# A two-layer hybrid decoder trunk: queries scaled with the keys, exchanged halves read in one product, paired Y tiles, a new order of steps

## The chip, the cores and the metric

One core of one Trainium2 chip runs the whole program. The time is the device time of one execution in microseconds; three executions of the kernel before are given by their median. Work is spread over TensorE (PE), VectorE (DVE), ScalarE (ACT), GpSimd (POOL) and SyncE (SP, which issues most DMAs). Each has its own instruction stream and works it off in the order in which the program was written.

## What is computed

Two layers on x (512 x 1024, float32). Each mixes tokens by three attentions of one normalised input and then channels by a gated convolution block:

```python
for i in range(DEPTH):                                   # DEPTH = 2
    h = rms_norm(x, attn_norm[i])
    qa, ka, va, qb, kb, vb, qc, kc, vc, gates = split(h @ w_in[i])
    # q and k of A, B, C: rms_norm per head, then rotary:
    #   concat([x1 * c - x2 * s, x2 * c + x1 * s])
    ya = moba_attention(qa, ka, va)                      # 4 heads of 64
    yb = sliding_window_sink_attention(qb, kb, vb, sinks[i])   # 8 heads on 2 kv heads
    yc = differential_attention(qc, kc, vc, lam, subln)  # 4 heads, two softmax maps of 32
    g = sigmoid(gates.reshape(B, S, 3, D))
    merged = g[..., 0, :] * (ya @ w_pa) + g[..., 1, :] * (yb @ w_pb) + g[..., 2, :] * (yc @ w_pc)
    x = x + merged @ w_out[i]
    h = rms_norm(x, mlp_norm[i])
    u = causal_depthwise_conv(h @ w_up[i], conv_w[i], conv_b[i])   # width 3
    gate_u, val_u = split(u, 2)                          # 2816 each
    x = x + (silu(gate_u) * val_u) @ w_down[i]
```

## The kernel before

**Products.** A float32 product of activations and weights is made as three products of reduced operands: each side is split into a high part and the rest, and high x high, high x rest and rest x high are summed. A weight tile of 128x1024 comes by DMA into one of two `raw` buffers; ACT casts it to `whi`, and DVE (one instruction) or POOL (four pieces of 256) subtracts to get `wlo` (`w_prep`, L639). The tile's `raw` buffer is free for the next transfer when both are done. Activations have the same two parts, `h0k` and `h1k` for k = 0 to 7. PE sums into one of four PSUM banks `d`; two banks `tp` take transposes and attention outputs, two banks `s` scores.

**Stages of a layer.** A list `ORDER` (layer 0) or `ORDER1` (layer 1) orders the blocks of dense products of the attention half: `Q` for a branch's q, k and v columns (blocks qk of 4 tiles and v of 2), `g` for half a gate (4 tiles), `p` for half an output projection. Then come the two halves of w_out, eleven `up` blocks (4 tiles each, with convolution and SiLU at their evacuation) and two `down` blocks of 11 tiles. "vC" below is branch C's v block, "gC0" the first half of C's gate, and a number behind a dot is the layer.

**Attention.** For each branch the projected q and k are rotated, scaled and split (`prep`, L903, with `rope`, L887), transposed on PE, multiplied to scores, masked, exponentiated (`soft`, L1073), transposed again, multiplied with v, and gathered into Y tiles (`gather`, L1230), the left side of the projections. Between these steps data goes PE, PSUM, ACT or DVE, PE.

**Who runs when.** The program is a set of generators ("threads"), each asking for its next step on one engine. A planner (`Estimate`, from L177, and the loop at the end of `trunk`) keeps a clock per engine from a table of durations and picks, step by step, the thread that goes on; threads have priorities (`P_...`). The dense blocks are the thread of lowest priority and fill PE where no attention step is ready. So every constant at the head of the file and every entry of the cost table moves instructions.

**Normalisation.** A branch that stands in `ORDER` ahead of the first gate works on the input before it is normalised, and its outputs are scaled at evacuation by `rn`, the reciprocal norms (`RAW_BR`). Behind the last of them `renorm` (L583) makes the normalised parts: for each k a DVE product, an ACT cast to `h0k` and a DVE subtraction to `h1k`. They overwrite the parts that the raw branches read. In the same way the first `up` block reads un-normalised h; its outputs get a row of reciprocal norms `ROW` at evacuation (`evac_up`, L1391, where the product is written back into the PSUM bank), while `renorm` makes the parts for the ten others.

**Softmax.** `rstd_tb` (L799) makes reciprocal norms of q and k on POOL: `RS` and `NRS` for q (with the score scale and its negative), `RK` for k. k is scaled by `RK` after rotary, q is not: its scale goes into the exponential, exp(RS * s + nb), with nb = NRS * max(s).

Of the kernel before, what the change touches and what calls it, by code (L numbers as in the profile page):

```python
# [26 lines left out]
LOCK = True  # L27
ORDER = ('QC', 'QA', 'gC0', 'QB', 'gC1', 'gA0', 'gA1', 'pC0', 'gB0', 'pC1', 'pA0', 'gB1', 'pA1', 'pB0', 'pB1')
CAP = 3
POOL_LEAD = 2.5  # L30
POOL_BIAS = -1000000000.0
RAWUP = 1
RENORM = 1.5
EXTRA = ({'C': 0, 'A': 6, 'B': 0}, {'C': 13, 'A': 3, 'B': 35})
GROOM = (0, 4)
PRING = 3
UNPARK = 6
PTMAX = 6
QUOTA = (6, 6)
HURRY = 1  # L40
P_HURRY = 2
P_SCORE = 4.5
P_TRANS = 2.5
P_VALUE = 3.4
P_SOFT = 1.9
P_SPREAD = 0.2
P_GATHER = 0.7
P_SUBLN = 0.7
P_SQUASH = 2.1
P_MOVE = 3.6  # L50
P_PREP = 5
TOL = 0.05
COPY = 0.2
SCALE = 1
# [5 lines left out]
MAJ_OUT = 3  # L60
MAJ_DOWN = 0
MAJ_LAST = 3
FINE = 1
SPILL = 8

# [108 lines left out]
class Estimate:  # L174
    SEM = 0.16

    def __init__(self):  # L177
        self.clock = {"PE": 0.0, "ACT": 0.0, "DVE": 0.0, "POOL": 0.0, "SP": 0.3, "DGE": 0.0, "DMA": 0.0}
        self.table = None
        self.mode = None  # L180
        self.written = {}
        self.used = {}
        self.pred = {}
        self.rings = {}
        self.lock = LOCK
        self.port = {"DVE": deque(maxlen=24), "POOL": deque(maxlen=24)}
# [52 lines left out]
    def note(self, key, op, args, kw):
# [9 lines left out]
        ins = [x for x in aps if not any(x is o for o in outs)]  # L249
        t = self.clock[key]  # L250
        for x in ins:
            t = max(t, self.written.get(x.tensor.name, 0.0) + self.SEM)
        for o in outs:
            nm = o.tensor.name
            if key != "PE" and op != "dma_start":
                t = max(t, self.written.get(nm, 0.0) + (self.SEM if nm in self.written else 0.0))
            if nm[:2] in ("h0", "h1"):
                t = max(t, self.used.get(nm, 0.0) + self.SEM)
            if nm in self.pred:
                t = max(t, self.used.get(self.pred.pop(nm), 0.0) + self.SEM)  # L260
        if op == "dma_start":
# [5 lines left out]
        else:  # L267
            two = False
            if self.lock and key in ("DVE", "POOL"):
# [6 lines left out]
            if two:  # L276
                for s, e in self.port["POOL" if key == "DVE" else "DVE"]:
                    if s <= t < e:
                        t = e
            end = t + self.cost(key, op, out, ins, kw, args)  # L280
            self.clock[key] = end
            if two:
                gap = 0.05 if key == "POOL" else 0.0
                self.port[key].append((t + gap, end - gap))
# [4 lines left out]
        for o in outs:  # L289
            self.written[o.tensor.name] = max(self.written.get(o.tensor.name, 0.0), end)  # L290
# [40 lines left out]
def trunk(ctx: ExitStack, tc: tile.TileContext, out: bass.AP, a: dict):  # L331
# [448 lines left out]
    RW, SS, V, RS, NRS, RK, Y, SIG, M, MH = {}, {}, {}, {}, {}, {}, {}, {}, {}, {}  # L780

    def alloc_raw(br, l):
        RW[br] = [slots.get() for _ in range(2)]
        RK[br] = small.tile([128, TB, NK[br]], F32, name="rk" + br, bufs=1)
        RS[br] = small.tile([128, TB, NQ[br]], F32, name="rq" + br, bufs=1)
        NRS[br] = small.tile([128, TB, NQ[br]], F32, name="nrq" + br, bufs=1)
# [12 lines left out]
    def rstd_tb(br, t, g0, g1):  # L799
        nq = NQ[br]  # L800
        v = small.tile([128, 16], F32, name="vv", bufs=3)[:, :g1 - g0]
        nc.vector.tensor_scalar(v, SS[br][:, g0:g1], 1.0 / DH[br], EPS, op0=OP.mult, op1=OP.add)
        r = small.tile([128, 16], F32, name="rr", bufs=3)[:, :g1 - g0]
        nc.gpsimd.tensor_tensor(r, v, mhalf[:, :g1 - g0], op=OP.pow)
        sc = DH[br] ** -0.5
        if g0 < nq:
            nc.gpsimd.tensor_scalar(RS[br][:, t, :], r[:, :nq], sc, None, op0=OP.mult)
            nc.gpsimd.tensor_scalar(NRS[br][:, t, :], r[:, :nq], -sc, None, op0=OP.mult)
        if g1 > nq:
            nc.gpsimd.tensor_copy(RK[br][:, t, :], r[:, max(nq - g0, 0):])  # L810

    def evac_qk(br, key):
        def f(t, ps):
            if br in RAW_BR[key // 2]:
                nc.scalar.activation(raw_tb(br, t), ps, AF.Copy, scale=RN[key][:, t:t + 1])
            else:
                nc.scalar.copy(raw_tb(br, t), ps)
# [69 lines left out]
    def rope(br, t, sv, dv, mv, q0, q1):  # L887
# [8 lines left out]
        nc.vector.tensor_mul(mv[:, :, :, :h], sv[:, :, :, h:], tab(t2, 0, h))  # L896
# [760 lines left out]
```

## Time and profile before

| what | us |
|---|---|
| median of three runs | 1584.74 (1582.8 to 1584.83) |
| the profiled execution | 1583.99 |
| its span in the trace | 1582.1 |
| PE busy | 1544.0 |
| mean granted clock of PE | 0.999 of full speed |

The profiled execution is 0.75 us under the median. An instruction's row has its start and duration; in brackets stands how long its engine was idle before it and which operation released it. Every instruction carries the line of one helper (L168), so rows are told apart by tiles and shapes. A row of grouped instructions ends with the total idle time just before them. Matmuls overlap: the row of one 512-column matmul lasts some 0.39 us, but a new one can start before the last ends.

### The profile page before, as it was taken

To read this page: it belongs to the slowest core of one execution; us is meant where nothing else is said; L and a number is where in the kernel's file an instruction comes from. 1 tells how busy PE (TensorE), PEld (TensorE's weight loads), DVE (VectorE), ACT (ScalarE), POOL (GpSimd) and SP (SyncE) were. 2 spreads that over 40 slices of the span, in tenths; PEclk is the share of its full clock that TensorE was granted. 3 is DMA by queue.
4 is the path that set the end of the run, shared out by engine and by line. 5 is a ranking of instruction groups with operands and counts; after the bars stand their busy time and mean duration, and the time that the engine had idled before them with its cause. 6 is when DMAs were issued, how large, how long until landed. Compare 5 with 4: busy or idle time off the path is not lost.

```text
span 1582.1 us, 21228 instructions
## 1 busy us (share of the span) xinstructions
PE 1544.0 (98%) x7584; PEld 1281.9 (81%) x7584; DVE 1048.0 (66%) x2211; ACT 800.8 (51%) x1566; POOL 338.9 (21%) x455
## 2 busy tenths in 40 slices
PE   8999999999999999999999999999999999999999
PEld 6977888877878888888888787888888788888887
DVE  4798878887576665543249887887776855665231
ACT  7566686764444444333146666766734544444210
POOL 3465443431010000000034564443300200000000
PEclk9999999999999999999999999999999999999999
DMA  5522523214223333333332224322242233223331
GB/s 176 154 68 79 173 68 94 80 54 135 90 83 107 89 98 107 107 98 127 95 114 69 66 79 160 107 67 61 73 159 88 72 106 107 80 86 101 120 120 53
DMA packets 115496, 157.22 MB, mean 99 GB/s; under 512 B 18880, under 2 KB 71104, under 8 KB 115392
## 3 DMA queue, kind: packets, MB, share of 16 engines
q1 hardware_dynamic: 102768, 153.19, 31.3%
q10 hardware_dynamic: 12624, 2.69, 0.9%
q8 instruction: 60, 0.98, 0.3%
q14 instruction: 44, 0.36, 0.1%
HBM read 144.84 MB, written 11.01 MB: 99 GB/s over the span
## 4 chain that ended last, share of the span: by engine, by line
PE 77%; DVE 14%; ACT 4%; DMA 2%; POOL 2%; issue 1%; SPq 0%; ACTq 0%; DVEq 0%; POOLq 0%
PE d L168 70%; PE tp L168 6%; DVE slot L168 5%; DVE temp L168 4%; ACT slot L168 2%; PE s L168 1%; DVE h L168 1%; ACT whi L168 1%; DVE s L168 1%; DMA raw<-in_w_up 1%; DVE wlo L168 1%; POOL rr L168 1%; DVE nb L168 1%; DMA slot<-in_c_cs 0%; ACT h L168 0%
## 5 line engine op out<-in xcount | busy, mean ns | idle before, releaser
L168 PE MATMUL d<-h,whi 128*128 128x512 f32 x2176 | 681.2, 394 | 4.0 <-DVE temp L168 2.7
L168 PEld LDWEIGHTS d<-h,whi 128*128 128x128 f32 x2176 | 398.6, 188 | 84.5 <-ACT temp L168 5.4
L168 PE MATMUL d<-h,wlo 128*128 128x512 f32 x1088 | 424.8, 390 | 0.0
L168 ACT CAST whi<-raw 128x1024 fp32r<-128x1024 f32 x246 | 256.2, 1052 | 280.2 <-PE d L168 136.3
L168 DVE TENSOR_TENSOR wlo<-raw,whi 128x1024 fp32r<-128x1024 f32 x175 | 213.5, 1233 | 257.9 <-ACT whi L168 257.5
L168 POOL TENSOR_TENSOR wlo<-raw,whi 128x256 fp32r<-128x256 f32 x284 | 225.2, 823 | 351.9 <-ACT whi L168 315.2
L168 PE MATMUL d<-slot,whi 128*128 128x512 f32 x864 | 267.0, 390 | 0.0
L168 PEld LDWEIGHTS d<-h,wlo 128*128 128x128 f32 x1088 | 204.2, 188 | 44.0
L168 PE MATMUL d<-whi,h 128*128 128x512 f32 (+1 forms) x768 | 205.9, 346 | 0.6 <-ACT h L168 0.6
L168 PEld LDWEIGHTS d<-slot,whi 128*128 128x128 f32 x864 | 161.1, 188 | 32.8
L168 DVE SCALAR_TENSOR_TENSOR temp<-d,packed,temp 128x511 f32<-128x511 f32 (+1 forms) x176 | 127.8, 747 | 63.4 <-ACT temp L168 60.3
L168 PE MATMUL d<-slot,wlo 128*128 128x512 f32 x432 | 168.2, 389 | 0.0
L168 PEld LDWEIGHTS d<-whi,h 128*128 128x128 f32 x768 | 134.8, 192 | 15.8 <-ACT h L168 1.0
L168 ACT CAST slot<-tp 128x256 fp32r<-128x256 f32 (+4 forms) x308 | 108.2, 379 | 70.8 <-PE tp L168 64.6
L168 PE MATMUL d<-wlo,h 128*128 128x256 f32 (+1 forms) x384 | 131.1, 341 | 0.2 <-DVE wlo L168 0.2
L168 ACT ACTIVATE temp<-d,packed 128x512 f32<-128x512 f32 x88 | 67.9, 773 | 86.1 <-PE d L168 79.4
L168 PE MATMUL d<-whi,slot 128*128 128x512 f32 x352 | 108.6, 389 | 0.0
L168 POOL TENSOR_TENSOR rn<-nvs,mhalf 128x4 f32<-128x4 f32 x3 | 3.0, 1008 | 482.4 <-DVE nvs L168 482.4
L168 DVE TENSOR_TENSOR slot<-slot,d 128x512 f32<-128x512 f32 x80 | 54.6, 685 | 73.9 <-PE d L168 71.2
L168 PEld LDWEIGHTS d<-slot,wlo 128*128 128x128 f32 x432 | 81.1, 188 | 17.0
L168 DVE TENSOR_TENSOR slot<-tp,slot 64x128 fp32r<-64x128 f32 (+4 forms) x180 | 76.0, 425 | 25.7 <-ACT slot L168 24.1
L168 ACT CAST slot<-temp 128x256 fp32r<-128x256 f32 (+2 forms) x140 | 58.1, 454 | 56.7 <-DVE temp L168 56.5
(113 smaller groups left out, 1784.8 us busy)
## 6 DMA issues: line engine op xcount, KB each, us to landing
raw<-in_w_up SPq DMA_DIRECT2D x176, 256.0 KB, 3.4
raw<-in_w_in SPq DMA_DIRECT2D x82, 512.0 KB, 3.7
raw<-in_w_down SPq DMA_DIRECT2D x44, 512.0 KB, 3.9
raw<-in_w_out SPq DMA_DIRECT2D x16, 512.0 KB, 4.6
x_spill<-slot SPq DMA_DIRECT2D x8, 512.0 KB, 3.9
b_parked<-slot SPq DMA_DIRECT2D x8, 512.0 KB, 5.3
slot<-b_parked SPq DMA_DIRECT2D x8, 512.0 KB, 5.8
raw<-in_w_pb SPq DMA_DIRECT2D x8, 512.0 KB, 3.7
```

The source lines that it names most:

```text
L168: r = f(*args, **kw)
```

## The change

1. **Reciprocal norms.** `RS`, `NRS` and `RK` become one tile `RQK`, written by the power on POOL itself. q is scaled together with k after rotary, in one wider product. The masked reduction of scores gives nb directly (with a factor -sqrt(dh) and a minimum), so that the product that made nb goes, and the exponential's scale is the constant -1.
2. **Rotary.** The two products of exchanged halves become one that reads the halves in exchanged order; q and k are evacuated in an arrangement of parts for it.
3. **Y tiles of B** are paired so that each of two evacuations of `gather` moves 64x2x128 where four moved 64x128.
4. **First up block.** The row product goes to an SBUF slot (`UR`) and not back into the PSUM bank; the activation and the convolution's two steps read the slot.
5. **Differential scale.** Where DVE scales the second map, reciprocal and lambda are applied in one instruction.
6. **Planner.** Latencies per engine, ready times by parts of a tile, other costs, and other constants and orders. Ahead of the first gate now stands only C, so the normalised parts are made between vC and gC0 in both layers.

```diff
-ORDER = ('QC', 'QA', 'gC0', 'QB', 'gC1', 'gA0', 'gA1', 'pC0', 'gB0', 'pC1', 'pA0', 'gB1', 'pA1', 'pB0', 'pB1')
-CAP = 3
+ORDER = ('QC', 'gC0', 'QA', 'gA0', 'QB', 'gC1', 'gA1', 'pC0', 'pC1', 'gB0', 'pA0', 'pA1', 'gB1', 'pB0', 'pB1')
+CAP = 4
...
-RENORM = 1.5
+RENORM = 0.5
...
-TOL = 0.05
+TOL = -0.2
...
-ORDER1 = ('QC', 'QA', 'gC0', 'QB', 'gC1', 'pC0', 'gA0', 'pC1', 'gB0', 'gA1', 'gB1', 'pA0', 'pA1', 'pB0', 'pB1')
+ORDER1 = ('QC', 'gC0', 'QA', 'gC1', 'QB', 'gA0', 'pC0', 'pC1', 'gA1', 'gB0', 'pA0', 'gB1', 'pA1', 'pB0', 'pB1')
...
-    SEM = 0.16
+    SEM = {"PE": 0.08, "ACT": 0.05, "DVE": 0.034, "POOL": 0.08, "SP": 0.1}
+    LAG = {"PE": 0.163, "ACT": 0.1, "DVE": 0.084, "POOL": 0.045}
...
-        r = small.tile([128, 16], F32, name="rr", bufs=3)[:, :g1 - g0]
-        nc.gpsimd.tensor_tensor(r, v, mhalf[:, :g1 - g0], op=OP.pow)
-        sc = DH[br] ** -0.5
-        if g0 < nq:
-            nc.gpsimd.tensor_scalar(RS[br][:, t, :], r[:, :nq], sc, None, op0=OP.mult)
-            nc.gpsimd.tensor_scalar(NRS[br][:, t, :], r[:, :nq], -sc, None, op0=OP.mult)
-        if g1 > nq:
-            nc.gpsimd.tensor_copy(RK[br][:, t, :], r[:, max(nq - g0, 0):])
...
+        nc.gpsimd.tensor_tensor(o, v.rearrange("p (q n) -> p q n", n=h),
+                                mhalf[:, :g1 - g0].rearrange("p (q n) -> p q n", n=h), op=OP.pow)
...
-        nc.vector.tensor_mul(mv[:, :, :, :h], sv[:, :, :, h:], tab(t2, 0, h))
-        nc.vector.tensor_mul(mv[:, :, :, h:], sv[:, :, :, :h], tab(t2, h, 2 * h))
+        x = bass.AP(tensor=sv.tensor, offset=sv.offset + h,
+                    ap=[list(sv.ap[0]), [2 * h, (q1 - q0) * n], [-h, 2], [1, h]])
+        nc.vector.tensor_mul(mv, x, tab(t2, 0, 2 * h))
...
-            nc.vector.tensor_mul(kv, kv, RK[br][:, t, p * nk:(p + 1) * nk, None].to_broadcast([128, nk, d]))
+            if br == "B":
+                r5 = rot[:, :320].rearrange("p (n d) -> p n d", d=d)
+                nc.vector.tensor_mul(r5, r5, RQK[br][:, t, p, :, None].to_broadcast([128, 5, d]))
+            else:
+                r4 = rot[:, :256].rearrange("p (q n d) -> p q n d", q=2, d=d)
+                nc.vector.tensor_mul(r4, r4, RQK[br][:, t, :, p * nk:(p + 1) * nk, None].to_broadcast([128, 2, nk, d]))
...
-                nc.vector.tensor_tensor_reduce(s_, s_, mask, 1.0, -3e38, OP.add, OP.max, job["mx"][:, m:m + 1])
-            nb = job["nb"][:, m0:m1]
-            nc.vector.tensor_mul(nb, job["mx"][:, m0:m1], NRS[br][:, t, g0 + m0:g0 + m1])
+                nc.vector.tensor_tensor_reduce(s_, s_, mask, -DH[br] ** 0.5, 3e38, OP.add, OP.min, job["nb"][:, m:m + 1])
...
-                                     scale=RS[br][:, t, g0 + m:g0 + m + 1], accum_out=job["den"][:, m:m + 1])
+                                     scale=-1.0, accum_out=job["den"][:, m:m + 1])
...
-            for i in range(4 if br == "B" else 2):
...
+            for i in range(2):
+                r = slice(i * 64, i * 64 + 64)
+                if br == "B":
+                    x = ps.rearrange("p (a i c) -> p a i c", a=2, i=2)[r, :, i, :]
+                    dst.append((two(Y[br][2 * p])[r, :, sl], two(Y[br][2 * p + 1])[r, :, sl], x))
...
             if blk < RAWUP:
-                nc.vector.tensor_mul(ps, ps, ROW[2 * l + 1][:, :512])
+                if c % 2 == 0:
+                    UR[c // 2] = slots.get()
+                r = UR[c // 2][:, (c % 2) * 512:(c % 2) * 512 + 512]
+                nc.vector.tensor_mul(r, ps, ROW[2 * l + 1][:, :512])
+                ps = r
```

TensorE has the same number of instructions before and after, 7558. VectorE's go from 2209 to 1985, ScalarE's from 1417 to 1369, GpSimd's from 460 to 380. Three places show how the streams move. A name is the tile's with a running number; `mx`, `nb` are the softmax's maximum and bias, `temp` and `slot` working tiles.

ScalarE at the end of vC in layer 0, before: behind the four evacuations of v (`slot21_22 <- d, rn`) stand the casts of two weight tiles and the evacuation of vA.

```order
L168 ACTIVATE slot21_22_524<-d_526,rn_129 128x256
L168 COPY slot23_24_602<-tp1_10_519 128x512
L168 ACTIVATE slot21_22_524<-d_539,rn_129 128x256
L168 ACTIVATE slot21_22_524<-d_552,rn_129 128x256
L168 ACTIVATE slot21_22_524<-d_565,rn_129 128x256
L168 CAST whi_643<-raw_502 128x1024
L168 CAST whi_709<-raw_583 128x1024
L168 ACTIVATE slot26_27_655<-d_657,rn_129 128x256
L168 ACTIVATE slot26_27_655<-d_670,rn_129 128x256
```

VectorE at the same place, before: the rest of v, one weight tile, then branch C's rotary.

```order
L168 SCALAR_TENSOR_TENSOR slot22_23_525<-d_565,rn_129,slot21_22_524 128x256
L168 TENSOR_TENSOR wlo_644<-raw_502,whi_643 128x1024
L168 TENSOR_TENSOR temp3_7_726<-slot11_12_201,slot16_17_504 128x256
L168 TENSOR_TENSOR temp1_8_727<-slot11_12_201,slot16_17_504 128x8x16 x2
L168 TENSOR_TENSOR temp3_7_726<-temp3_7_726,temp1_8_727 128x256
L168 TENSOR_TENSOR temp3_7_726<-temp3_7_726,rkC_203 128x128
```

The same place after, first on ScalarE, then on VectorE. Behind the four evacuations stand the cast of one weight tile and those to `h00` and the following parts:

```order
L169 ACTIVATE slot21_22_506<-d_508,rn_129 128x256
L169 ACTIVATE slot21_22_506<-d_521,rn_129 128x256
L169 ACTIVATE slot21_22_506<-d_534,rn_129 128x256
L169 ACTIVATE slot21_22_506<-d_547,rn_129 128x256
L169 CAST whi_633<-raw_484 128x1024
L169 CAST h00_113<-slot24_25_606 128x512
L169 CAST h01_114<-slot25_26_608 128x512
L169 CAST h02_115<-slot26_27_618 128x512
L169 CAST h03_116<-slot27_28_626 128x512
```

```order
L169 SCALAR_TENSOR_TENSOR slot22_23_507<-d_547,rn_129,slot21_22_506 128x256
L169 TENSOR_TENSOR wlo_634<-raw_484,whi_633 128x1024
L169 TENSOR_TENSOR h10_121<-slot24_25_606,h00_113 128x512
L169 TENSOR_TENSOR h11_122<-slot25_26_608,h01_114 128x512
L169 TENSOR_TENSOR h12_123<-slot26_27_618,h02_115 128x512
```

What moved: the casts to `h00` and on, and the subtractions to `h10` and on, which gC0's first matmuls read, came twenty and more rows later before, and now stand directly at vC's end.

ScalarE between the first and second up block of layer 0, before and after. `whi` is the cast of a weight tile, `h05` to `h07` the casts of the normalised parts; `slot` are the block's outputs.

```order
L168 CAST slot27_208_5134<-temp1_67_5090 128x512
L168 CAST slot13_209_5137<-temp2_68_5100 128x512
L168 CAST whi_5140<-raw_5035 128x1024
L168 CAST h05_4646<-slot17_207_5082 128x512
L168 CAST whi_5183<-raw_5077 128x1024
L168 CAST h06_4647<-slot29_210_5172 128x512
L168 CAST h07_4648<-slot10_211_5178 128x512
L168 CAST whi_5219<-raw_5147 128x1024
```

```order
L169 CAST slot23_210_4902<-temp3_67_4855 128x512
L169 CAST slot29_211_4905<-temp2_68_4866 128x512
L169 CAST whi_4908<-raw_4802 128x1024
L169 CAST whi_4947<-raw_4842 128x1024
L169 CAST whi_4982<-raw_4915 128x1024
L169 CAST h06_4412<-slot18_212_4966 128x512
L169 CAST h07_4413<-slot17_213_4974 128x512
L169 CAST whi_5015<-raw_4951 128x1024
```

What moved: `h06` and `h07` stood ahead of the cast of the third block's first tile, `whi_5219`; now they stand behind its counterpart, `whi_4982`, whose `raw` buffer is the one that POOL's `wlo_4909` (the third tile of the second block) frees.

VectorE in a softmax of branch C in layer 0, before and after (`ISA` is the masked reduction, followed by its write of the row value):

```order
L168 ISA s0_1_881,mx2_878<-s0_1_881,mfull_86 128x128
L168 ISA mx2_878 128x1
L168 TENSOR_TENSOR nb2_879<-mx2_878,nrqC_205 128x1
L168 ISA s1_2_883,mx2_878<-s1_2_883,mfull_86 128x128
L168 ISA mx2_878 128x1
L168 TENSOR_TENSOR nb2_879<-mx2_878,nrqC_205 128x1
```

```order
L169 TENSOR_TENSOR temp3_13_811<-temp3_13_811,rqkC_203 128x256
L169 ISA s0_1_825,nb2_823<-s0_1_825,mfull_86 128x128
L169 ISA nb2_823 128x1
L169 ISA s1_2_827,nb2_823<-s1_2_827,mfull_86 128x128
L169 ISA nb2_823 128x1
```

What moved: the product that made `nb` is no longer between the reductions and the exponential, and the scaling ahead of them is twice as wide.

## Rows read from the trace of the kernel before

**Rows 1.** Part 1 of the page: busy time of each engine, share, instructions.
```profile
PE 1544.0 (98%) x7584; PEld 1281.9 (81%) x7584; DVE 1048.0 (66%) x2211; ACT 800.8 (51%) x1566; POOL 338.9 (21%) x455
```

**Rows 2.** Windows: length, busy PE, PEld, DVE, ACT, POOL; clock, DMA, GB/s.
```profile
39.00:94.00 55.00, 51.03 (x342) 45.45 (x341) 42.89 (x113) 30.70 (x74) 26.00 (x34) 1.00 0.46 134
94.00:366.00 272.00, 264.31 (x1428) 220.30 (x1428) 233.65 (x682) 184.92 (x455) 123.34 (x171) 0.99 0.30 88
...
797.00:844.00 47.00, 46.11 (x310) 42.23 (x309) 25.82 (x50) 21.48 (x40) 21.33 (x29) 1.00 0.37 107
844.00:874.00 30.00, 28.16 (x147) 22.54 (x146) 29.07 (x80) 20.69 (x52) 13.89 (x17) 1.00 0.26 72
874.00:1144.00 270.00, 262.77 (x1416) 217.87 (x1415) 220.28 (x650) 187.39 (x460) 125.57 (x172) 1.00 0.29 87
```

**Rows 3.** Waits of PE: who released it, us in total, times, longest.
```profile
PE tp L168 <- DVE slot L168: 16.9, 26, 2.9
...
PE d L168 <- DVE temp L168: 2.7, 4, 1.0
```

**Rows 4.** Groups by operation and shape: busy, mean ns | idle before, released by.
```profile
L168 PE MATMUL tp<-identf,slot 128*128 128x128 f32 x352 | 55.6, 277 | 8.9 <-DVE slot L168 7.4 <-DVE nss L168 1.0 <-ACT slot L168 0.3
...
L168 DVE TENSOR_TENSOR temp<-slot,slot 128x128 f32<-128x128 f32 x96 | 38.9, 446 | 0.0
...
L168 PE MATMUL tp<-identr,slot 128*128 128x128 f32 x320 | 37.7, 240 | 3.1 <-DVE slot L168 2.1 <-ACT slot L168 0.6
...
L168 DVE TENSOR_TENSOR temp<-slot,slot 128x256 f32<-128x256 f32 x48 | 25.8, 537 | 1.1 <-POOL slot L168 1.1
...
L168 DVE TENSOR_TENSOR nb<-mx,nrqC 128x1 f32<-128x1 f32 x64 | 14.6, 227 | 2.2
...
L168 DVE TENSOR_TENSOR nb<-mx,nrqB 128x2 f32<-128x2 f32 x32 | 8.2, 257 | 1.1
...
L168 PE MATMUL tp<-onesr,slot 128*128 128x2 f32 x32 | 4.1, 243 | 2.0 <-DVE slot L168 2.0
```

**Rows 5.** Same view: the operations that prepare weights, h and v.
```profile
L168 ACT CAST whi<-raw 128x1024 fp32r<-128x1024 f32 x246 | 256.2, 1052 | 280.2 <-PE d L168 136.3 <-DMA raw<-in_w_up 94.7 <-DMA raw<-in_w_down 28.4
...
L168 DVE TENSOR_TENSOR wlo<-raw,whi 128x1024 fp32r<-128x1024 f32 x175 | 213.5, 1233 | 257.9 <-ACT whi L168 257.5
...
L168 DVE TENSOR_TENSOR h<-slot,h 128x512 fp32r<-128x512 f32 x32 | 23.9, 773 | 5.7 <-ACT h L168 5.7
...
L168 ACT CAST h<-slot 128x512 fp32r<-128x512 f32 x32 | 19.5, 623 | 7.7 <-DVE slot L168 7.6
...
L168 ACT ACTIVATE slot<-d,rn 128x256 fp32r<-128x256 f32 x16 | 7.6, 474 | 16.8 <-PE d L168 16.8
```

**Rows 6.** Timeline of PE, layer 0, at gC0's first matmuls: start, duration.
```profile
94.04 0.61 PE L168 MATMUL d<-h,whi 128*128 128x512 f32 x2
94.49 0.39 PE L168 MATMUL d<-h,wlo 128*128 128x512 f32 x1
```

**Rows 7.** Timelines of PE, POOL, ACT around layer 0's first up block.
```profile
456.82 0.70 PE L168 MATMUL d<-h,whi 128*128 128x512 f32 x2 [0.43 <-DVE temp L168]
...
463.70 4.88 POOL L168 TENSOR_TENSOR wlo<-raw,whi 128x256 fp32r<-128x256 f32 x4 [23.73 <-ACT whi L168]
...
464.93 1.15 ACT L168 CAST h<-slot 128x512 fp32r<-128x512 f32 x2
472.39 1.05 ACT L168 CAST whi<-raw 128x1024 fp32r<-128x1024 f32 x1 [6.31 <-DMA raw<-in_w_up]
```

**Rows 8.** Timeline of PE, layer 1, in the second up block.
```profile
1253.60 0.49 PE L168 MATMUL d<-h,whi 128*128 128x512 f32 x1 [0.76 <-ACT h L168]
```

**Rows 9.** Short windows, columns as in rows 2; the granted clock follows POOL.
```profile
82.00:86.00 4.00, 1.09 (x6) 0.87 (x6) 3.86 (x15) 2.08 (x7) 0.00 (x0) 1.00 0.43 131
...
152.00:154.00 2.00, 2.00 (x6) 1.54 (x5) 1.18 (x4) 2.00 (x6) 1.31 (x4) 0.50 0.00 0
...
150.00:157.00 7.00, 7.00 (x39) 6.24 (x39) 5.42 (x20) 5.66 (x13) 5.25 (x7) 0.76 0.20 69
```

More of the change, by code (lines that the diff above doesn't have):

```diff
@@ L181, in __init__ @@
         self.written = {}
+        self.parts = {}
         self.used = {}
@@ L198, in alloc_ready, with ready, box, when @@
         return self.used.get(ring[i], 0.0) if i >= 0 else 0.0
-    def ready(self, t):
-        return self.written.get(t.tensor.name, 0.0) + self.SEM
+    def ready(self, t, key="PE"):
+        return self.written.get(t.tensor.name, 0.0) + self.SEM.get(key, 0.05)
+    @staticmethod
+    def box(x):
+        ap = x.ap
+        row = ap[0][0]
+        f = x.offset % row if row else x.offset
+        p = x.offset // row if row else 0
+        return p, p + ap[0][1], f, f + 1 + sum(abs(st) * (c - 1) for st, c in ap[1:])
+    def when(self, x, key):
+        parts = self.parts.get(x.tensor.name)
+        if not parts:
+            return 0.0
+        p0, p1, f0, f1 = self.box(x)
+        t = 0.0
+        for (a, b, c, d), k, e in parts:
+            if c < f1 and f0 < d:
+                t = max(t, e + (0.01 if k == key else self.SEM[key]))
+        return t
     def cost(self, key, op, out, ins, kw, args):
@@ L205, in cost @@
         psum = any(x.space == bass.MemoryType.PSUM for x in (out, *ins))
+        lag = self.LAG[key]
         if key == "PE":
@@ L268, in note @@
             two = False
-            if self.lock and key in ("DVE", "POOL"):
+            if key in ("DVE", "POOL"):
                 sb = [x.space != bass.MemoryType.PSUM for x in ins if x.free_size() > 1]
@@ L275, in note @@
                                           and out.space != bass.MemoryType.PSUM)
-            if two:
-                for s, e in self.port["POOL" if key == "DVE" else "DVE"]:
+            if two and key == "POOL":
+                for s, e in self.port["DVE"]:
                     if s <= t < e:
                         t = e
[L280 to L284, printed above, removed]
+            elif two:
+                for x in self.port["POOL"]:
+                    if x[0] <= t < x[1]:
+                        t = x[1]
+                        break
+            c, lag = self.cost(key, op, out, ins, kw, args)
+            self.clock[key] = t + c
+            end = t + c + lag
+            if two and key == "POOL":
+                self.port[key].append([t, t + c, out.tensor.name, self.box(out)])
+            elif two:
+                self.port[key].append((t, t + c))
+                self.push(t, t + c)
         self.last = (t, end)
@@ L289, in note @@
         for o in outs:
-            self.written[o.tensor.name] = max(self.written.get(o.tensor.name, 0.0), end)
+            nm = o.tensor.name
+            self.written[nm] = max(self.written.get(nm, 0.0), end)
+            p0, p1, f0, f1 = box = self.box(o)
+            keep = [y for y in self.parts.get(nm, ()) if not (p0 <= y[0][0] and y[0][1] <= p1 and f0 <= y[0][2] and y[0][3] <= f1)]
+            keep.append((box, key, end))
+            self.parts[nm] = keep
 class Thread:
@@ L1113, in soft @@
             if br == "C":
-                rl = small.tile([128, 1], F32, name="rl")
-                nc.vector.tensor_mul(rl, rec[:, 1:2], lam[:, l:l + 1])
-                scale_any(P[:, 1, :w], P[:, 1, :w], rl)
+                if est.clock["ACT"] + SCALE <= est.clock["DVE"]:
+                    rl = small.tile([128, 1], F32, name="rl")
+                    nc.vector.tensor_mul(rl, rec[:, 1:2], lam[:, l:l + 1])
+                    nc.scalar.activation(P[:, 1, :w], P[:, 1, :w], AF.Copy, scale=rl)
+                else:
+                    nc.vector.tensor_scalar(P[:, 1, :w], P[:, 1, :w], rec[:, 1:2], lam[:, l:l + 1], op0=OP.mult, op1=OP.mult)
                 yield "DVE", [P], None
@@ L1386, in trunk @@
     CV = {}
+    UR = {}
     def p_act(k, i):
@@ L1584, in trunk @@
         best = None
+        if est.mode and est.mode[0]:
+            for r, th in pes:
+                if th.cur[0] == "PEt" and r <= now + BATCH:
+                    best = (max(now, r), th)
+                    break
         for r, th in pes:
-            if r <= now + TOL:
+            if best is None and r <= now + TOL:
                 best = (now, th)
```

141 lines of the change are left out of this document (83 added, 58 removed).

## The prediction

> **What bounds the kernel now.** I read the page's busy times first: PE is busy 1544.0 of 1582.1 us [rows 1], and it has the same 7558 instructions before and after. So the change can win only from PE's idle time, some 38 us, and lose by adding to it. Next come the windows by stage: outside the attention halves PE has next to no gap. Inside them it is idle 55 - 51.03 = 3.97, 272 - 264.31 = 7.69, .89, 1.84 and 7.23 us, 21.6 us together [rows 2], while VectorE is busy there 42.89 + 233.65 + 25.82 + 29.07 + 220.28 = 551.7 us of 674. Of PE's waits by releaser the largest is a `tp` bank's operand that VectorE writes late, 16.9 us in 26 waits [rows 3]. The groups say which: transposes of probabilities and of rotated q and k, and the small products of branch C's normalisation, idle 8.9 + 3.1 + 2.0 us before them [rows 4]. These waits end chains in which VectorE works for PE: rotary and scaling, then transpose; reduction, exponential, reciprocal, scaling, then transpose.
>
> Idle time in the trace is not the whole of a wait. A 512-column matmul lasts .39 but two of them start .45 apart, .225 each [rows 6], so a wait shows some .16 us less than it costs.
>
> **Part 1, the attention's waits: -15.5 us.** Removed on VectorE: the multiplications that make nb, in C and B alone 14.6 + 8.2 us [rows 4], and the halves of rotary, 96 x 446 ns by 48 x 537 ns, 42.8 - 25.8 = 17.0 us [rows 4]. The wider key scaling takes some back and the paired Y tiles give some; I let these cancel. That is 40 of 551.7 us of its work in these windows, 7%, and .23 to .26 us less in each softmax's own chain. The planner's new costs and order choose what fills the gaps. Of the visible 21.6 us, 1.0 is the program's start before the first product, so 8.9 - 1.0 + 3.1 + 2.0 = 13.0 us stand on chains that shorten; with .16 us for each of some 17 of them 15.7 us. The other 8.6 us (values, scores, evacuations) stand on chains that don't. The trace can't show what a planner gives. Its bounds: -2 us, if the waits only go to other places (a chain's .23 us on a few of them), and -22 us, if they all go. I take 80% of 15.7 (12.5), 20% of 8.6 plus hidden parts (2.2), and half of the 1.7 us that the clock took once: from 150 to 157 us PE was granted .76, and in 152 to 154 .50, the lower of the two levels (1.2 and 2.4 GHz); 7 x .24 = 1.7 us [rows 9]. The value is nearer the upper bound than the lower, since most of the waiting is behind VectorE [rows 3], and its queue is what shrinks.
>
> **Part 2, normalised parts between vC and gC0: +8.2 us.** Before, gC0's first matmul came at 94.04 without a wait [rows 6], its operands long made beside vA and qkA. Now they stand behind vC's last matmul. The chain after its end, by mean durations [rows 5]: ScalarE evacuates v (.474), casts a weight tile (1.052) and casts `h00` (.623), so the first matmul can start at about 2.2 to 2.4. VectorE's rest of v fits in beside this, and its weight subtraction starts behind ScalarE's weight cast: 1.53 + 1.233 = 2.76; then `h10` .773 to 3.5 and `h11` .773 to 4.3, with latencies 4.4. The matmul that reads `h11` is the fifth and would stand at 4 x .225 = .9. Later parts come every .77 us, faster than the six matmuls of each k need them. So PE loses 4.4 - .9 = 3.5 us in each layer, 7.0. In layer 1 six of the norm's products and four of rotary's stand on VectorE ahead of `h12`; I add 1.2 us. Queued behind these on VectorE is branch C's rotary, which now comes later against PE's end of vC; gC0's 96 products of .225, 21.6 us, cover it. Bounds: 7.0 (no extra in layer 1) and 10.5 (both layers with the extra, and 1.0 of slack in the starts). Nothing is removed here, so no gain: before there was no wait at this place.
>
> **Part 3, first to second up block: +1.5 us.** PE's waits for the `d` banks after the first block's row product, 2.7 us in 4 waits [rows 3], one of them .43 us at 456.82 [rows 7], with .16 each 3.3 us, go: the bank is free after the product. In layer 1 `h06` came late, .76 us [rows 8] and as much again in smaller waits, 1.5 together; total 4.8. What is late next: ScalarE's casts of `h06` and `h07` now stand behind the cast of the third block's first tile. That tile's buffer is freed by POOL's four pieces, 463.70 to 468.58, and its cast before started at 472.39 after 6.31 us of waiting for its DMA [rows 7]; the `h` casts at 464.93 were ahead of it and waited for nothing. At the same place in the new order `h06` is cast at 473.4, ready at 474.1, and `h16` another .773 and a latency later, 475.1. Without its bank waits PE would start the second block at 454.9 (456.82 less the wait of .6 in all and six matmuls of .225) and its fourth tile, three times 24 matmuls later, at 471.1. So a new wait of 3.0 us for `h06` and some .6 more for `h16`, 3.5 in each layer, stands against what went: 7.0 - 4.8 = 2.2; I take off .7 since the `d` banks' earlier release lets the transfer come sooner. Bounds: -4.8 (the weight tile comes in time) and +4 (PE waits for `h17` too).
>
> **Part 4, nothing.** The program's start and qkC of layer 0 keep their order on each engine; the tail, the down blocks and `MAJ_OUT` and `MAJ_LAST` move products inside blocks whose windows have no idle time. POOL's removed instructions lie on an engine busy 21% [rows 1]; as cover PE has its dense blocks, and without them a norm's chain would be shorter by about one small POOL operation. The wider evacuations of Y are fewer and longer at about equal sum.
>
> **Sum.** -15.5 + 8.2 + 1.5 = -5.8 us. Of the profiled execution, 1583.99 (span 1582.1 and 1.9 around it), that gives 1578.2; it is .75 us below the median, so against the median of 1584.74 it is 1579.0.
>
> **Rivals.**
> *The waits only move.* The order is the planner's, and the distance between a chain's producer and consumer, filled with dense work, is no longer in the new order than in the old; a shorter chain may then only wait at the next step. Then part 1 is -2 and the sum is +7.7: 1592.4. It decides for slower where the relief is under 8.2 + 1.5 - 3.2 = 6.5 us (3.2 is .2% of the time). For it: the two new waits are certain by the order, the relief is not. Against it: 40 us leave the queue that PE waits for.
> *Half relief.* Part 1 gives 9 us: +.7, 1585.4, no change that can be told.
> *Deep relief.* Nearly all waits go (-22) and the up block's casts come in time (part 3 between -4.8 and +1.5): -22 + 8.2 - 2 = -15.8, about 1569, between 1566 and 1572.
> *The clock answers the new waits.* PE stands still for 3.5 us in each layer and its clock falls. Once the trace shows that: .50 in 152 to 154 us; and once not: 82 to 86 us, with PE busy 1.09 of 4 us, kept 1.00 [rows 9]. A drop as that from 150 to 157 costs 1.7; twice that is +3.4: 1582.4.
> The Trainium skill, page "TensorE: Matmul & The Clock Gate", section "HAM oscillation — how this bites in real kernels", says that idle gaps in TensorE's work bring its clock down again. By that rule both new stalls would be answered by the lower clock, the time of this rival; the trace agrees at 152 and differs at 82 to 86.
>
> **How the numbers follow.** Forecast .42, only moving .20, half relief .12, deep .18, clock .08. The predicted time is the forecast's, 1579.0. Its own range, by parts 2 and 3, is 1574 to 1585. The range for 8 in 10 reaches down to the deep case's low side, 1567, and up to the first rival's time, 1592, where about half of its chance is left out. A measurement of this kernel can tell .2%, 3.2 us, from no change: same is 1581.6 to 1587.9. Faster: .36 of the forecast, .18 of deep, .03 of the clock's case: .57. Same: .06, .11, .03 of these, and .01 of the first rival: .21. Slower: .19 and the rest, .22.
>
> **What would show it.** In the profile after: PE's waits for `tp` from VectorE fall from 16.9 to about 4 us (part 1), or stay above 10 (first rival). At gC0's start in both layers PE waits, first for `h` by ScalarE, then by VectorE, 3.5 us or more together (part 2). The four waits for `d` from VectorE's `temp` are gone, and in the second up block's last tile PE waits about 3.5 us for `h` from ScalarE (part 3). The granted clock stays 1.00 behind both (forecast) or falls to .50 (clock). The prediction is wrong in its sign if the attention windows' idle time stays near 21.6 us, and in its reasons if that falls but gC0's start shows no wait.

## The result

The changed kernel takes 1595.4 us (median of four runs, 1593.9 to 1596.7) against 1584.6 of the kernel before: a ratio of 1.0073, interval 1.006 to 1.0085. It is slower by 10.8 us, where 5.8 less were forecast, and it lies above the range. The profiled execution took 1595.38, its span 1593.5 us. Of e1's six executions one took 3027.66 us and is left out below, so that e1 stands at 1579.2 us where the expectations name 1579.9.

The busy times of the page after answer to [rows 1]:

```profile
PE 1547.0 (97%) x7584; PEld 1288.7 (81%) x7584; DVE 1016.0 (64%) x1987; ACT 775.4 (49%) x1518; POOL 318.6 (20%) x375
```

PE's waits by releaser after (in total, times, longest) answer to [rows 3]:

```profile
PE tp L169 <- DVE slot L169: 14.8, 15, 3.8
PE d L169 <- ACT h L169: 10.2, 5, 3.2
...
PE d L169 <- DVE h L169: 4.3, 6, 1.1
```

VectorE's work fell by 32 us. Yet PE's waits for it at the transposes went only from 16.9 to 14.8 us, in fewer and longer pieces, and waits for the normalised parts `h`, from ScalarE and VectorE, stand at 14.5 us. The groups after answer to [rows 4]; the idle time before the first rose from 8.9 to 15.1 us, that before the second fell from 3.1 to 1.2:

```profile
L169 PE MATMUL tp<-identf,slot 128*128 128x128 f32 x352 | 55.7, 279 | 15.1 <-DVE slot L169 11.7 <-ACT slot L169 1.9 <-DVE nss L169 1.0
...
L169 PE MATMUL tp<-identr,slot 128*128 128x128 f32 x320 | 37.1, 243 | 1.2 <-DVE slot L169 0.6 <-ACT slot L169 0.2 <-DVE vs L169 0.2
```

At gC0's start in layer 0 stand the two waits that part 2 of the prediction worked out; timelines of PE, ScalarE and VectorE, start and duration first:

```profile
52.92 0.50 PE L169 MATMUL d<-h,whi 128*128 128x512 f32 x1 [2.02 <-ACT h L169]
54.47 0.50 PE L169 MATMUL d<-h,whi 128*128 128x512 f32 x1 [1.05 <-DVE h L169]
...
50.94 0.47 ACT L169 ACTIVATE slot<-d,rn 128x256 fp32r<-128x256 f32 x1 [0.96 <-PE d L169]
51.31 1.03 ACT L169 CAST whi<-raw 128x1024 fp32r<-128x1024 f32 x1
52.25 2.18 ACT L169 CAST h<-slot 128x512 fp32r<-128x512 f32 x4
...
52.61 1.21 DVE L169 TENSOR_TENSOR wlo<-raw,whi 128x1024 fp32r<-128x1024 f32 x1
53.74 2.48 DVE L169 TENSOR_TENSOR h<-slot,h 128x512 fp32r<-128x512 f32 x4
```

The chain is the one that was written down: evacuation of v, weight cast, cast to `h00`; weight subtraction, then `h10`. In layer 1 the same pair comes again, and two short waits behind it, for `h12` (.39 us) and `h13` (.18 us, at 847.76):

```profile
837.38 0.50 PE L169 MATMUL d<-h,whi 128*128 128x512 f32 x1 [2.02 <-ACT h L169]
838.85 0.50 PE L169 MATMUL d<-h,whi 128*128 128x512 f32 x1 [0.96 <-DVE h L169]
...
846.61 0.50 PE L169 MATMUL d<-h,whi 128*128 128x512 f32 x1 [0.39 <-DVE h L169]
```

In the second up block it is as part 3 had it, too: the third block's weight cast waits for its DMA, and the casts to `h06` and `h07` stand behind it. The last two rows are PE's at the same place in layer 1.

```profile
474.59 1.04 ACT L169 CAST whi<-raw 128x1024 fp32r<-128x1024 f32 x1 [7.39 <-DMA raw<-in_w_up]
475.54 1.14 ACT L169 CAST h<-slot 128x512 fp32r<-128x512 f32 x2
...
476.21 0.51 PE L169 MATMUL d<-h,whi 128*128 128x512 f32 x1 [1.96 <-ACT h L169]
477.55 0.50 PE L169 MATMUL d<-h,whi 128*128 128x512 f32 x1 [0.83 <-DVE h L169]
...
1262.51 0.49 PE L169 MATMUL d<-h,whi 128*128 128x512 f32 x1 [3.25 <-ACT h L169]
1263.85 0.79 PE L169 MATMUL d<-h,whi 128*128 128x512 f32 x1 [0.85 <-DVE h L169]
```

Behind each of these four places PE runs at half speed for a while. Windows, with the granted clock as the third number from the end; the last is for a fifth place, in the attention, and the row under it is the wait ahead of it:

```profile
54.00:56.00 2.00, 1.53 (x5) 1.22 (x6) 2.00 (x4) 0.42 (x1) 0.00 (x0) 0.76 0.48 65
56.00:58.00 2.00, 2.00 (x6) 1.57 (x5) 2.00 (x4) 1.04 (x2) 0.00 (x0) 0.50 1.00 347
58.00:60.00 2.00, 2.00 (x9) 1.60 (x8) 1.97 (x5) 1.95 (x4) 0.10 (x1) 0.89 0.30 121
478.00:480.00 2.00, 2.00 (x7) 1.58 (x6) 0.10 (x1) 0.44 (x1) 2.00 (x3) 0.57 0.81 250
480.00:482.00 2.00, 2.00 (x6) 1.53 (x6) 1.50 (x2) 0.34 (x1) 0.80 (x2) 0.58 0.07 16
840.00:842.00 2.00, 2.00 (x7) 1.56 (x6) 2.00 (x5) 1.82 (x3) 0.00 (x0) 0.52 0.58 220
1264.00:1266.00 2.00, 2.00 (x5) 1.61 (x6) 0.40 (x1) 0.00 (x0) 1.94 (x3) 0.50 0.76 226
242.00:250.00 8.00, 6.12 (x20) 5.05 (x21) 4.13 (x10) 7.08 (x9) 3.85 (x6) 0.57 0.37 124
...
243.88 1.09 PE L169 MATMUL tp<-identf,slot 128*128 128x128 f32 x4 [3.75 <-DVE slot L169]
```

One such place costs 2 x (.24 + .50 + .11) = 1.7 us, as much as the only one before, [rows 9]. A fifth drop follows a 3.75 us wait in the attention: 6.12 x .43 = 2.6 us. Together 4 x 1.7 + 2.6 = 9.4 us against 1.7.

Where the 11.4 us between the spans came from, by the starts of the first products of each stage in the two timelines:

| stage | before | after | difference |
|---|---|---|---|
| to the first product of qkC, layer 0 | 8.9 | 9.4 | +.5 |
| attention half, layer 0 | 377.5 | 380.6 | +3.1 |
| first three up blocks, layer 0 | 70.9 | 72.7 | +1.8 |
| attention half, layer 1 | 370.3 | 374.7 | +4.4 |
| first three up blocks, layer 1 | 73.4 | 74.9 | +1.6 |

All other stages agree within .1 us. Read by causes: the two places at gC0 cost 6.6 us of visible idle time in six waits and some .16 hidden in each, 7.6. The clock costs 9.4 - 1.7 = 7.7, of which 3.4 are the whole of what the up blocks lost. The attention halves lost 7.5; gC0 took 7.6 and the clock 4.3, so they gained 4.4 elsewhere. The sum is .5 + 7.6 + 7.7 - 4.4 = 11.4.

### The profile page after: what moved, and what is told of

Read it like the earlier page. It is cut to its first block, busy times and chain, and to the rows that moved or that the text cites. A ratio compares the mean times of both kernels' runs of the same rounds, so it can differ in the third digit from the quotient of the medians.

```text
span 1593.5 us, 20883 instructions
## 1 busy us (share of the span) xinstructions
PE 1547.0 (97%) x7584; PEld 1288.7 (81%) x7584; DVE 1016.0 (64%) x1987; ACT 775.4 (49%) x1518; POOL 318.6 (20%) x375
## 4 chain that ended last, share of the span: by engine, by line
PE 82%; DVE 11%; ACT 3%; issue 1%; DMA 1%; POOL 1%; SPq 0%; ACTq 0%; POOLq 0%; DVEq 0%
PE d L169 74%; PE tp L169 6%; DVE slot L169 4%; DVE temp L169 4%; ACT slot L169 2%; PE s L169 1%; DVE s L169 1%; ACT whi L169 1%; DVE h L169 1%; DVE nb L169 1%; DMA raw<-in_w_up 0%; DMA slot<-in_c_cs 0%; DVE wlo L169 0%; POOL wlo L169 0%; DMA raw<-in_w_in 0%
## 5 line engine op out<-in xcount | busy, mean ns | idle before, releaser
L169 PEld LDWEIGHTS d<-h,whi 128*128 128x128 f32 x2176 | 403.5, 190 | 96.0 <-ACT h L169 10.5
L169 POOL TENSOR_TENSOR wlo<-raw,whi 128x256 fp32r<-128x256 f32 x276 | 220.6, 830 | 375.1 <-ACT whi L169 314.5
L169 DVE SCALAR_TENSOR_TENSOR temp<-d,packed,temp 128x511 f32<-128x511 f32 (+1 forms) x160 | 116.2, 747 | 71.8 <-ACT temp L169 68.9
L169 ACT CAST slot<-tp 128x256 fp32r<-128x256 f32 (+5 forms) x264 | 98.8, 405 | 74.7 <-PE tp L169 69.7
L169 ACT ACTIVATE temp<-d,packed 128x512 f32<-128x512 f32 x80 | 61.8, 773 | 87.8 <-PE d L169 87.8
L169 DVE TENSOR_TENSOR slot<-tp,slot 128x512 fp32r<-128x512 f32 (+5 forms) x148 | 70.9, 484 | 42.8 <-ACT slot L169 41.9
L169 PEld LDWEIGHTS d<-slot,wlo 128*128 128x128 f32 x432 | 81.1, 188 | 16.9
```

The costliest lines, as they stand in the source:

```text
L169: r = f(*args, **kw)
```

## The experiments

The kernel before was run again beside each set of runs and took 1584.0 to 1584.4 us.

**The change in two parts.** The first run has parts 1 to 5 under the old planner and orders, the second part 6 under the old arithmetic:

```diff
 e1: the kernel before
+    parts 1 to 5 of the change
 e2: the kernel before
+    part 6 (class Estimate, the loop's PEt and BATCH, all constants, ORDER, ORDER1)
```

> The kernel before with parts 1 to 5 of the change (scaling of q with k, one product for the exchanged halves, paired Y tiles, row product to an SBUF slot, one instruction for the differential scale) and none of part 6: old planner, old constants, old orders. Theory 'order' (the loss of 10.8 us comes from part 6, which makes the normalised parts behind vC, and PE's clock falls after the waits there; the shorter chains by themselves save a little): 1578 to 1584. Rival 'arithmetic' (the wider key scaling or the row product lengthens what PE waits for): 1590 or more.

> The kernel before with part 6 alone: new planner, constants and orders, old arithmetic. Theory 'order': 1595 to 1600, with the two waits of 3.4 us at gC0 and a clock of .5 behind them. Rival 'arithmetic': 1584 to 1588.

Measured: e1 1579.2 (ratio .9968, .9954 to .9981), e2 1603.3 (1.0116, 1.0101 to 1.0131). The arithmetic saves 5.2 us in the old order of things; the new plan costs 18.9 under the old arithmetic, over its expectation, and 16.2 under the new. In e2 the clock cost 15.6 us counted as above: behind a wait of 6.80 us and shorter ones after it stands the longest stay at half speed of all profiles; PE's timeline and a window of e2:

```profile
1072.25 1.52 PE L169 MATMUL tp<-slot,slot 128*128 128x512 f32 x2 [6.80 <-ACT slot L169]
...
1068.00:1090.00 22.00, 13.75 (x47) 10.78 (x48) 17.86 (x72) 15.38 (x39) 1.63 (x3) 0.53 0.07 24
```

So the change's loss is in part 6.

**gC0 behind QA.**

```diff
-ORDER = ('QC', 'gC0', 'QA', 'gA0', ...
+ORDER = ('QC', 'QA', 'gC0', 'gA0', ...
-ORDER1 = ('QC', 'gC0', 'QA', 'gC1', ...
+ORDER1 = ('QC', 'QA', 'gC0', 'gC1', ...
```

> The changed kernel, only gC0 put back behind QA in both orders, so that the normalised parts are made beside vA and qkA. Theory 'order': the waits at gC0 (7.4 us) go and with them two clock drops of 1.7 us: 1595.4 - 10.8 = 1584.6. Rival 'planner' (what goes there comes back as waits at other steps, since the rest was laid out for the new order): 1592 or more.

Measured: 1582.4 (.9984, .9975 to .9994), 13.0 us under the changed kernel and even a little faster than before. The waits at gC0 are gone (the `h` that is left belongs to the up blocks), and those for VectorE at the transposes are a third of the changed kernel's, while a few for ScalarE have grown. The clock's share did not go with them, as the theory had it: e3's profile has five places at half speed, too (from 121, 271, 473, 1029 and 1251 us), which cost some 9.1 us counted as above, and the mean granted clock is .993 against .994. So the 13 us are hardly the clock's: of the 12.6 us between the two spans (1593.5 and 1580.9) 7.9 are idle time of PE, and 12.4 lie in the attention halves. PE's waits in e3:

```profile
PE tp L169 <- ACT slot L169: 6.9, 4, 4.8
PE d L169 <- ACT h L169: 5.7, 3, 3.2
...
PE tp L169 <- DVE slot L169: 5.2, 6, 1.7
```

Whether these 13 us belong to the place itself or to it with the new constants was asked the other way round, with gC0 ahead of QA under the old planner, once as in e1 and once as in e10 (below):

```diff
 e15: e1, e16: e10
-ORDER = ('QC', 'QA', 'gC0', ...      (and ORDER1)
+ORDER = ('QC', 'gC0', 'QA', ...
```

> The run e1 (parts 1 to 5, old planner; 1579.9) with gC0 put ahead of QA in both orders and nothing else. Theory 'place' (the normalised parts behind vC cost 7.4 us of waits and up to 3.4 of clock under any planner): 1587 to 1591, with the two waits of 2.0 and 1.0 us at each gC0. Rival 'fit' (gC0's place costs only together with the new constants, 13 us there): within 3 us of 1579.9.

> The run e10 (parts 1 to 5, old planner, TOL 0; 1574.0) with gC0 put ahead of QA in both orders. Theory 'place': 1581 to 1586. Rival 'fit': within 3 us of 1574.0.

Measured: e15 1591.8 (12.6 over e1), e16 1581.4 (7.4 over e10). The place costs under either planner, 7.4 to 13.0 us; e15 a little more than was expected of it.

**The clock behind the waits.** Products that nobody reads, on PE alone, in the stretch where it would wait; ScalarE's and VectorE's work is untouched:

```diff
+        if b.norm % 2 == 0 and i == 0 and b.norm not in filled:      # gC0, ahead of its first product
+            for _ in range(15):
+                nc.tensor._eng.matmul(ps[0], x[:, :128], y[:, :512], start=True, stop=True)
+        if b.norm % 2 == 1 and i == 3 and b.norm not in filled:      # second up block, ahead of its fourth tile
...
+            for _ in range(16):
```

> The changed kernel with products of weights by weights that nobody reads, put on PE where it waits: 15 ahead of gC0's first product in each layer, 16 ahead of the fourth tile of the second up block in each layer. The order is otherwise the same. Theory 'clock' (PE's standing still at these four places takes its clock down, 1.7 us each): clock 1.00 behind all four, 1595.4 - 6.8 = 1588.6. Rival (the clock falls for another reason, or the products only add their own time): 1595 or more.

Measured: 1591.4 (1.0038, 1.0024 to 1.0053), 4.0 under the changed kernel, not 6.8. Windows of e5 at three of the four places, then at the fourth and at a place in the attention, and PE's waits ahead of these two:

```profile
52.00:60.00 8.00, 8.00 (x36) 6.47 (x35) 7.93 (x14) 5.41 (x10) 0.58 (x1) 1.00 0.55 182
470.00:486.00 16.00, 16.00 (x73) 13.23 (x72) 9.43 (x14) 7.39 (x11) 2.90 (x4) 1.00 0.44 131
1258.00:1270.00 12.00, 12.00 (x57) 9.93 (x56) 7.48 (x10) 7.30 (x10) 2.87 (x4) 1.00 0.46 144
846.00:848.00 2.00, 2.00 (x6) 1.52 (x6) 1.97 (x3) 0.00 (x0) 2.00 (x4) 0.50 0.34 57
1030.00:1032.00 2.00, 2.00 (x9) 1.51 (x7) 2.00 (x6) 0.00 (x0) 0.00 (x0) 0.50 0.84 227
...
844.43 0.50 PE L169 MATMUL d<-h,whi 128*128 128x512 f32 x1 [1.97 <-DVE h L169]
1027.95 0.63 PE L169 MATMUL tp<-identf,slot 128*128 128x128 f32 x4 [2.36 <-DVE slot L169]
```

At three places the clock stays at 1.00 where it had fallen behind the wait: work that nobody needs, put into a wait, made the kernel faster. At gC0 of layer 1 a wait of 1.97 us came later, for `h12`, with its own drop. A further drop stands at 145 us, where the changed kernel has none. In all, e5's four drops cost 6.8 us against 9.4, and this accounts for nearly all of the 2.7 us between the two profiled spans (1590.8 and 1593.5). And at 1028 a wait that the changed kernel has too, 2.49 us there and 2.36 here, is followed by .50 here and by 1.00 there; the changed kernel:

```profile
1029.67 0.63 PE L169 MATMUL tp<-identf,slot 128*128 128x128 f32 x4 [2.49 <-DVE slot L169]
...
1030.00:1036.00 6.00, 6.00 (x34) 5.04 (x33) 5.34 (x11) 2.19 (x4) 2.48 (x5) 1.00 0.29 87
```

So a wait of 2 to 3 us may bring the clock down or not; what decides stays open. It is not the program alone: e5's five executions had mean clocks of .995 to .999 and took 1592.8 to 1586.9 us.

**The first up block.** Two edits that leave all 7558 TensorE instructions in the changed kernel's sequence: the row product back in its bank (e6), or the product in its slot and the weights of the third block prepared later, so that the casts to `h06` and `h07` come first (e9):

```diff
 e6
-                r = UR[c // 2][:, (c % 2) * 512:(c % 2) * 512 + 512]
-                nc.vector.tensor_mul(r, ps, ROW[2 * l + 1][:, :512])
-                ps = r
+                nc.vector.tensor_mul(ps, ps, ROW[2 * l + 1][:, :512])
 e9
-                pump(b.t0 + g[-1] + (3 if len(g) == 1 else 1))
+                lead = b.t0 + g[-1] + (3 if len(g) == 1 else 1)
+                pump(min(lead, b.t0 + 4) if b.norm is not None and b.norm % 2 and b.id in UP1 and g[-1] < 3 else lead)
```

> The changed kernel with part 4 alone undone: the first up block's row product is written back into its PSUM bank. TensorE's order is the same instruction by instruction; the casts to h06 and h07 come ahead of the third block's first weight tile again. Theory 'queue' (part 4 costs time since those casts stand behind a weight tile whose transfer is late): the up blocks lose 6.5 us as in the run with the new planner and the old arithmetic, in place of 13.1, so 1595.4 - 6.5 = 1589. Rival 'bank' (the waits for the bank that come back cost as much, clock included): 1594 or more.

> The changed kernel, part 4 kept, but the third up block's first two weight tiles are prepared one to two tiles later, so that the casts to h06 and h07 stand ahead of them. TensorE's order is the same. Theory 'queue': the wait of 3 us for h06 and h16 goes in both layers with its clock drop, 2 x (3.2 + 1.7) and little in its place: 1595.4 - 9.8 = 1585.6, and it beats the row product in place by the bank waits (3 us). Rival (the weight tiles themselves come late in the third block, or the clock falls there all the same): 1592 or more.

Measured: e6 1588.1 (7.3 under the changed kernel, 6.5 expected), e9 1587.2 (8.2, 9.8 expected). That e9 beats e6 by 3 us is not shown; .9 lies within the noise. ScalarE's and PE's timelines of e9, layer 0, show the casts ahead of the weight and of PE's waits only one left, for a bank:

```profile
470.35 0.62 ACT L169 CAST h<-slot 128x512 fp32r<-128x512 f32 x1 [0.58 <-DVE slot L169]
473.75 1.05 ACT L169 CAST whi<-raw 128x1024 fp32r<-128x1024 f32 x1 [2.78 <-DMA raw<-in_w_up]
...
479.74 0.70 PE L169 MATMUL d<-h,whi 128*128 128x512 f32 x2 [1.08 <-DVE temp L169]
```

Part 4 is thus worth less than nothing as it stands, by the place of two casts of .6 us in ScalarE's queue. In e6 the waits at gC0 are the changed kernel's, yet in the profiled execution, 2.9 us under e6's median, the clock stays at 1.00 behind those of layer 0:

```profile
52.45 0.49 PE L169 MATMUL d<-h,whi 128*128 128x512 f32 x1 [2.02 <-ACT h L169]
...
52.00:60.00 8.00, 6.61 (x28) 5.27 (x29) 7.93 (x14) 5.29 (x9) 0.69 (x1) 1.00 0.51 174
```

**What an order is worth.** To see how far the times hang on the order alone, one tolerance of the planner was changed, once under the old arithmetic and once under parts 1 to 5:

```diff
 e8: the kernel before, e10: e1
-TOL = 0.05
+TOL = 0.0
 e13: the kernel before, e14: e1
-TOL = 0.05
+TOL = 0.02
```

> The kernel before with one constant of the planner changed that is about no piece of the work (TOL 0.05 to 0): a new order, 5633 of 7558 TensorE instructions in the same sequence as before. It measures what a new order alone does. Theory 'planner' (the sum of waits depends on the order by several us either way, so that a part's effect is seen only under several orders): between 1579 and 1595, off 1584.4 by over 2. Rival (orders of one planner are alike): within 2 us of 1584.4.

> Parts 1 to 5 with the old planner, as in the run e1, with the same constant changed (TOL 0): the third pair of old and new arithmetic. Theory 'order' (the arithmetic itself saves 4 to 8 us under any order): 4 to 8 us under the run e8. Rival (the 4.5 us of e1 were the luck of its order): within 2 us of e8, or over it.

> The kernel before with TOL 0.02 in place of 0.05: another new order of the old arithmetic (6315 of 7558 TensorE instructions in the same sequence). Theory 'planner' (the order before was a lucky one among many, and a new order of the old arithmetic costs several us): 1588 to 1604. Rival (e8 was an exception): 1580 to 1588.

> Parts 1 to 5 with the old planner and TOL 0.02: the fourth pair of old and new arithmetic. Theory 'order' (the arithmetic saves 4 us or more under any order): at least 4 us under e13. Rival (it saves only by the luck of an order): within 2 us of e13 or over it.

Measured, with PE's waits for VectorE at the `tp` banks from each profile in brackets:

| planner | old arithmetic | parts 1 to 5 | difference |
|---|---|---|---|
| old, TOL .05 | before, 1584.4 (16.9) | e1, 1579.2 (7.6) | -5.2 |
| old, TOL 0 | e8, 1603.7 (14.2) | e10, 1574.0 (7.3) | -29.7 |
| old, TOL .02 | e13, 1596.1 (17.0) | e14, 1578.5 (6.9) | -17.6 |
| new | e2, 1603.3 (12.5) | after, 1595.4 (14.8) | -7.9 |

PE's waits of e8:

```profile
PE tp L168 <- DVE slot L168: 14.2, 12, 4.5
PE s L168 <- ACT slot L168: 12.4, 9, 4.6
```

and of e10:

```profile
PE tp L168 <- DVE slot L168: 7.3, 10, 3.3
PE tp L168 <- DMA temp<-in_chans: 5.7, 1, 5.7
PE d L168 <- DVE h L168: 4.6, 4, 2.0
PE s L168 <- ACT slot L168: 3.3, 5, 0.9
```

A window of e8 stands behind one of its waits, PE at .57 for 12 us:

```profile
354.00:366.00 12.00, 6.96 (x33) 6.12 (x31) 7.94 (x33) 7.01 (x22) 0.78 (x2) 0.57 0.61 218
```

Two expectations were missed: e8 lies 8.7 us above its range, and e10 is 29.7 us under e8, not 4 to 8. Under the old planner the arithmetic cuts that wait by about half or more in all three orders. The old arithmetic spreads over 1584 to 1604 us and stands lowest in the order that it came with; the new one lies within 1574 to 1579. The mean of the three differences is -17.5. The clock is not the whole of the spread: counted as above it cost 1.7 us in the kernel before, 8.4 in e8 and 5.7 in e13.

**Both repairs, and the best version.** e12 is the changed kernel with gC0 behind QA and the casts first; e11 is e10 with the weights of the second and third up block prepared later:

```diff
 e11: e10
-                pump(b.t0 + g[-1] + (3 if len(g) == 1 else 1))
+                lead = b.t0 + g[-1] + (3 if len(g) == 1 else 1)
+                pump(min(lead, b.t0 + max(3, g[-1] + 2)) if b.id in UP1 and g[-1] < 3 else lead)
```

> The changed kernel with both repairs: gC0 behind QA (as in e3) and the casts to h06 and h07 ahead of the third up block's weights (as in e9). If the two losses are separate places, their gains add: 1595.4 - 13.0 - 8.2 = 1574.2. Rival (the clock and the order make them one loss): 1580 or more.

> The run e10 (parts 1 to 5 with the old planner, TOL 0: 1574.0) with the second up block's fourth weight tile and the third block's first ones prepared one to two tiles later, so that the casts to h05, h06 and h07 and the subtraction to h15 stand ahead of them; TensorE's order is the same. In e10 TensorE waited 2.0 us at this place in each layer. Theory 'queue': these 4 us go, 1570.0, and with one clock drop in layer 1 1568.5. Rival (the weight tiles are late in their place): 1574 or more.

Measured: e12 1573.3 (.9934, .9919 to .9949), e11 1570.3 (.9916, .9901 to .993). The two gains add (1574.2 expected), so they are two losses at two places. e11 beats the kernel before by 13.7 us and the changed one by 25.1; its waits for `h` at that place are all but gone, one of 1.8 us for a bank stands in their place in layer 0 and one of 1.1 in layer 1, and its clock falls at one place where e10's fell at two.

## Why the prediction was wrong

*Part 1, the attention's waits* (-15.5): the first step that failed. The changed kernel gained 4.4 us there, not 14.7 (both without the clock's share). The sign that the prediction named for its own error stands in the trace: in the windows of the attention PE is idle 12.17 + 15.05 = 27.2 us against 21.6 before, and still 20.6 without the six waits at gC0.

```profile
39.00:370.00 331.00, 318.83 (x1774) 269.43 (x1773) 257.59 (x676) 203.63 (x513) 139.97 (x171) 0.98 0.32 95
803.00:1154.00 351.00, 335.95 (x1867) 283.39 (x1866) 266.72 (x682) 212.06 (x514) 149.04 (x173) 1.00 0.29 88
```

The reason given was sound: the chains are shorter and VectorE's queue too (32 us less work, 40 were counted), and three pairs under the old planner show the transposes' wait for VectorE fall from 14 to 17 us to about 7. What failed was the step from shorter chains to the waits under this order, four fifths of which were taken to go whatever the planner made of it. The saving belongs to arithmetic and order together: it was 5.2, 29.7 and 17.6 us under three old orders and 7.9 under the new one. By the starts of the first products, and without the clock, the two attention halves (w_out included) took 833.1 us before, 836.1 in the changed kernel, 824.3 in e3, 825.5 in e1 and 821.0 in e10. So with gC0 behind QA the relief was 8 to 12 us, still under 14.7. The order before was, by luck, a low one for the old arithmetic: two other values of one tolerance put it 12 and 19 us higher. Why the changed kernel keeps 14.8 us of waits for VectorE is open. Under the new planner they are 5.2 with gC0 behind QA (e3), but 10.5 in e12; under the old planner with gC0 ahead they are 6.8 (e15) and 4.7 (e16). So neither the place nor the planner does it alone.

*Part 2, gC0* (+8.2): right in chain and near in size, 7.6 us. In the trace the second product waited, for `h10`, and `h11` was in time; layer 1's extra was .57 us of visible idle time and not 1.2. But this is not the whole price of the place: putting gC0 back gives 13.0 us, the rest in the attention halves, which the forecast had not tied to it, and hardly by the clock.

*Part 3, the up blocks* (+1.5): the mechanism was right, a wait of 2.8 us visible in layer 0 and 4.1 in layer 1. Without the clock the stage lost nothing, .0 against +1.5; with it 3.4.

*The clock*: the second step that failed. It was forecast as a gain of .85, and as a rival with a chance of .08 at +3.4. It cost 7.7. All four new waits were followed by half speed in the profiled execution, and the drop at 150 had cost exactly what each of them cost. The rule that the prediction cited from the Trainium skill, page "TensorE: Matmul & The Clock Gate", section "HAM oscillation — how this bites in real kernels", was the better guide at these four; the windows at 82 [rows 9] and 1030 show that it is no certainty for every such wait. I had read one counter-example as a reason to give it a twelfth of the chance.

Together the misses are 10.3 (part 1), 8.5 (the clock), -.6, -1.5 and .5 (the start), 17.2 us from -5.8 to +11.4.

*The first rival* (the waits only move, 1592.4) came nearest, and its condition held: the relief, 4.4, was under the 6.5 from which it decides. That a shorter chain waits at its next step, its reason, is not shown. It, too, left out the clock.

*Part 4, nothing*: held. The start differs by .5 us, and no other stage by .1.

## What to carry to other kernels

Where a planner sets the order, a part's saving is a property of part and order together: measure the arithmetic under the old order and under a few neighbours of it before the planner is fitted anew, for here one tolerance moved the time by 19 us. When a step is put directly behind the work whose buffers it overwrites, write down its chain by engine queue, since it stands whole on the path; and in a kernel bound by TensorE add to each new wait of some 2 us the 1.7 us that the clock may take behind it. What stands ahead of a short operation in its engine's queue matters more than the operation: two casts behind a late weight tile cost 8 us, the clock's share included.

## What was not expected of the hardware

PE's stay at half speed can be much longer than at the places that cost 1.7 us: in e2 PE had a mean clock of .53 for 22 us, with waits that followed each other, and in e8 .57 for 12 us. And products without use, put into waits of some 3 to 4 us, made the kernel 4 us faster (e5). The same wait was followed by half speed in one kernel and by full speed in another (52 us in the changed kernel and in e6; 1028 us in e5 and in the changed kernel); the runs don't show why, and executions of one kernel differ in it, too.
